# Scaling the handover blocks on DVE and ACT and turning them by transposes, in place of products with diag(factor)

## The chip, the cores and the metric

The kernel runs on one core of one Trainium2 chip. The metric is the device time of one execution in microseconds (us); several executions are taken and the median is given. Beside the timed runs there is one profiled execution, from which all rows of the profile come.

The engines by the names of the profile: PE is TensorE (matrix products), PEld its weight loads, DVE is VectorE, ACT is ScalarE, POOL is GpSimd, SP is SyncE, which here only issues DMAs. Each engine works through its own queue in order and waits on semaphores for the others.

## The reference

Two layers over 512 latent tokens and 256 context tokens of width 1024, all in float32. Layer 0 mixes tokens by retention, layer 1 by a gated linear recurrence (HGRN2); after each mixer comes a gated convolutional feed-forward. Around every one of these four sub-layers stands the same code, and the change lies only there:

```python
def rms_norm(x, g):
    xf = x.astype(jnp.float32)
    y = xf * lax.rsqrt(jnp.mean(xf * xf, -1, keepdims=True) + NORM_EPS)
    return (y * g.astype(jnp.float32)).astype(x.dtype)
...
        h_l = h_l + g1_l * rms_norm(y_l, norm_g[i, 1])
        u_l = rms_norm(h_l, norm_g[i, 2]) * (1.0 + sc2_l) + sh2_l
        h_l = h_l + g2_l * rms_norm(conv_ffn(u_l, ffn_w_up[i], ffn_conv_w[i], ffn_conv_b[i], ffn_w_down[i], True),
                                    norm_g[i, 3])
```

So the output y of a sub-layer is normalised, weighted and added to the stream h; then h is normalised again, scaled and shifted per channel, and is the input u of the next sub-layer.

## The kernel before

**Layout.** A sub-layer ends with tokens on the partitions: blocks of 128 tokens by 1024 channels. The next one needs its input u with channels on the partitions, as a sum of two float32r halves: hi (a rounded copy) and lo (the rest). Every large product is done three times (hi·hi, hi·lo, lo·hi).

**Handover.** The function `handover` is the bridge. It is used four times: after retention (called m0 in this document: 6 blocks, tiles named `trm`, `hxm`, `yr`, `um`), after the first feed-forward (e0: 6 blocks; `tre`, `hxe`, `yf`, `ue`), after the recurrence (m1: 4 blocks; again `trm`, `hxm`, and `yh`, `um`) and at the end (e1), which only writes the output and has no turn. In it `yb(b)` is the block of y in SBUF and `hb(b)` the block of the stream h.

For a block b, `norms` does, in this order: add the last partial product to y (DVE, L421), two sums of squares (ACT, L424), a reciprocal root r and one Newton step (ACT L428, DVE L142 to L144), y·r·gain (DVE, L448), h += y (DVE, L451) with a store of h to DRAM issued by POOL, the sum of squares of h (ACT, L452, which writes its squares over `yb`), the factor q by the same root and Newton step, and last the 128x128 matrix dg = diag(q) (DVE, L459).

For a pair of blocks, `turn` does four times (j = 0..3, two groups of 128 channels each): four float32 products of a 128x128 piece of `hb` with dg (PE, L475), which turn the piece and scale it by q at once, into one PSUM bank of 512 columns; two ACTs that apply the channel scale and shift out of PSUM (`mod`, L484) into a part of `yb`, whose content is no longer needed; hi (ACT, L491); lo (DVE, L492). The bank comes from a pool of two (`sml`), so group j waits until `mod` of group j-2 has read its bank.

**Order.** Around the handover, `tail` and `lead` put everything into one plan: the last products of the sub-layer that ends (PE, `tl`, L528), the norms and turns, the weight splits of the next sub-layer (ACT L585, DVE L589), and its first products (PE, `ld`, L121), which need all four lo of a pair. Each step carries an engine, an estimated cost, the steps that it needs, a rank and a slack. `Plan.run` plays this through once while the program is built: each engine takes, among the steps that its estimates call ready, the one of lowest rank. This fixes the order of instructions in the queues of PE, ACT and DVE; at run time they keep that order. A rank is a tuple: `(-1,)` goes ahead of all, `(-1, 9)` are the splits of the first weight half, then `(pr, stage)` of pair pr, `(1, 9)` the splits of the second half. On PE the turns have rank `(0,)`, the `tl` products rank 1, the `ld` products rank 2.

Of the kernel before, what the change touches and what calls it, by code (L numbers as in the profile page):

```python
# [9 lines left out]
F32 = mybir.dt.float32  # L10
F32R = mybir.dt.float32r
U8 = mybir.dt.uint8
AF = mybir.ActivationFunctionType
ALU = mybir.AluOpType

P = 128
# [22 lines left out]
class Plan:  # L39
# [5 lines left out]
    def add(self, eng, cost, deps, rank, emit, slack=0.0):  # L45
        self.steps.append(Step(eng, cost, list(deps), rank, emit, slack))
        return self.steps[-1]
# [22 lines left out]
class Net:  # L70
# [321 lines left out]
    def handover(self, nm, y, hsrc, gain, mods, u, hdst, nb, big, tmp):  # L392
        nc = self.nc
        per = y[0].shape[1]
        hx = [big([P, 3, D], F32, f"hx{nm}{j}") for j in range((nb + 2) // 3)]
        if nb % 3:
            g = hx[-1][:, 2:3]
        else:
            g = big([P, 3, D], F32, "gr" + nm)[:, 0:2]
        small = lambda n, w: self.cp.tile([P, w], F32, tag=f"sm{w}", name=f"{n}{nm}", bufs=12)  # L400
        rows = hsrc.rearrange("(b p) d -> p b d", p=P)
        for j, x in enumerate(hx):
            n = min(3, nb - 3 * j)
            nc.sync.dma_start(x[:, :n], rows[:, 3 * j : 3 * j + n])
        for v in range(g.shape[1]):
            nc.scalar.dma_start(g[:, v], self.gains[gain][v : v + 1].broadcast_to([P, D]))
        yb = lambda b: y[b // per][:, b % per]
        hb = lambda b: hx[b // 3][:, b % 3]
        if u is not None:
            A, B = mods()  # L410

        def norms(b, tails):
            ts, v, pr = slice(b * P, b * P + P), int(b >= 4), b // 2
            ss, r, q, dg = {}, {}, {}, {}
            add = self.plan.add
            half = lambda c: slice(c * 512, c * 512 + 512)

            def evac(c):
                if not c:
                    ss[0] = small(f"ss{b}", 4)  # L420
                nc.vector.tensor_tensor(yb(b)[:, half(c)], tails[c].ps, yb(b)[:, half(c)], ALU.add)  # L421

            def square(c):
                nc.scalar.activation(tmp(f"sq{nm}{b}{c}"), yb(b)[:, half(c)], AF.Square, accum_out=ss[0][:, c : c + 1])  # L424

            def start(d, x):
                d[0] = small(f"{'rq'[d is q]}{b}", 2)
                nc.scalar.activation(d[0][:, 0:1], x, AF.Abs_reciprocal_sqrt, bias=self.eps, scale=1.0 / D)  # L428

            sq = []  # L430
            for c in range(2):
                e = add("DVE", 0.67, [tails[c]], (pr, 0), lambda c=c: evac(c))
                tails[c].freed = e
                sq.append(add("ACT", 0.75, [e], (pr, 1), lambda c=c: square(c)))
            n = add("DVE", 0.16, sq, (-1,), lambda: nc.vector.tensor_tensor(ss[0][:, 2:3], ss[0][:, 0:1], ss[0][:, 1:2],
                                                                            ALU.add))
            n = add("ACT", 0.28, [n], (-1,), lambda: start(r, ss[0][:, 2:3]))
            n = add("DVE", 0.55, [n], (-1,), lambda: self.newton(r[0], ss[0][:, 2:3]))
            if u is None:
                for c in range(2):  # L440
                    cs = half(c)
                    n = add("DVE", 1.35, [n], (pr, 2), lambda cs=cs: (
                        nc.vector.scalar_tensor_tensor(yb(b)[:, cs], yb(b)[:, cs], r[0][:, 0:1], g[:, v, cs],  # L443
                                                       ALU.mult, ALU.mult),
                        nc.vector.tensor_tensor(hb(b)[:, cs], hb(b)[:, cs], yb(b)[:, cs], ALU.add),  # L445
                        (nc.sync, nc.scalar)[c].dma_start(hdst[ts, cs], hb(b)[:, cs])))
                return None
            n = add("DVE", 1.28, [n], (pr, 2), lambda: nc.vector.scalar_tensor_tensor(  # L448
                yb(b), yb(b), r[0][:, 0:1], g[:, v], ALU.mult, ALU.mult))
            n = add("DVE", 1.23, [n], (pr, 2), lambda: (  # L450
                nc.vector.tensor_tensor(hb(b), hb(b), yb(b), ALU.add), nc.gpsimd.dma_start(hdst[ts], hb(b))))  # L451
            n = add("ACT", 1.23, [n], (pr, 3), lambda: nc.scalar.activation(yb(b), hb(b), AF.Square,  # L452
                                                                           accum_out=ss[0][:, 3:4]))
            n = add("ACT", 0.28, [n], (-1,), lambda: start(q, ss[0][:, 3:4]))
            n = add("DVE", 0.55, [n], (-1,), lambda: self.newton(q[0], ss[0][:, 3:4]))

            def diag():
                dg[0] = self.cp.tile([P, P], F32, tag="diag", name=f"dg{nm}{b}", bufs=4)
                nc.vector.tensor_scalar(dg[0], self.ident, q[0][:, 0:1], None, ALU.mult)  # L459

            n = add("DVE", 0.25, [n], (-1,), diag)
            return n, dg

        def turn(pr, ready):
            add, v, cs = self.plan.add, int(pr == 2), slice(pr * W, pr * W + W)
            done = []
            for j in range(4):
                ps = {}

                def cross(j=j, ps=ps):  # L470
                    ps[0] = self.sml(f"tr{nm}{pr}{j}").rearrange("p (f t) -> p f t", f=2)
                    for f in range(2):
                        for z, (_, dg) in enumerate(ready):
                            k = 2 * j + f
                            nc.tensor.matmul(ps[0][:, f, z * P : z * P + P], hb(2 * pr + z)[:, k * P : k * P + P], dg[0],  # L475
                                             start=True, stop=True)

                x = yb(2 * pr + j // 2).rearrange("p (f t) -> p f t", f=4)[:, j % 2 * 2 : j % 2 * 2 + 2]
                hi, lo = (u[z + j // 2][:, j % 2 * 2 : j % 2 * 2 + 2, cs] for z in (0, 2))

                def mod(j=j, ps=ps, x=x):
                    for f in range(2):
                        k = 2 * j + f
                        nc.scalar.activation(x[:, f], ps[0][:, f], AF.Identity, scale=A[:, k, v : v + 1],  # L484
                                             bias=B[:, k, v : v + 1])

                prev = self.cross[-2:][:1] if len(self.cross) > 1 else []
                t = add("PE", 0.45, [n for n, _ in ready] + prev, (0,), cross, 1.0)
                m = add("ACT", 0.95, [t], (pr, 4), mod)
                self.cross.append(m)  # L490
                e = add("ACT", 0.62, [m], (pr, 5), lambda hi=hi, x=x: nc.scalar.activation(hi, x, AF.Copy))  # L491
                done.append(add("DVE", 0.67, [e], (pr, 6), lambda hi=hi, lo=lo, x=x: nc.vector.tensor_tensor(  # L492
                    lo, x, hi.bitcast(F32), ALU.subtract)))
            return done

        return norms, turn

    @staticmethod
# [939 lines left out]
```

## Time and profile before

| | us |
|---|---|
| timed runs | 2173.55, 2172.46, 2169.12 |
| median | 2172.46 |
| profiled execution | 2173.22 |
| its span in the profile | 2171.5 |
| busy: PE / DVE / ACT / POOL | 2113.8 / 1337.2 / 830.5 / 303.8 |

The span is the time from the first to the last recorded instruction; the execution's own time has 1.7 us more around it. The three handovers with a turn lie at about 676 to 747 us (m0), 1255 to 1326 us (e0) and 1755 to 1806 us (m1). In the profile one float32 product appears as two records on PE, so the 128 products of L475 are 256 records. "Idle before" in a row is the time in which the engine stood still just before those instructions, with the one that released it.

### The profile page before, as it was taken

The page shows a single profiled execution, that of the slowest core. Times are in us where ns is not written, and L with a number is a line of the kernel's source. Part 1 is how long each engine was busy: PE and PEld are TensorE (multiplying, and loading weights), DVE is VectorE, ACT ScalarE, POOL GpSimd, SP SyncE. Part 2 cuts the span into 40 slices and gives each one's busy share as a digit, 9 for nine tenths or more (in the row PEclk, how much of TensorE's full clock was granted, in tenths as well). Part 3 has the DMA queues.
Part 4 walks back from the last instruction along what each step waited for, and adds up shares of the span by engine and source line. Part 5 has one row for each costly group of instructions (what it writes and reads, how often), then busy time and mean ns, then how long its engine had stood idle before and what let it go on. Part 6 is the DMA issues. An engine that isn't in the chain of part 4 may idle for free. (4 is left out here: it accounts for less than half of the span.)

```text
span 2171.5 us, 31001 instructions
## 1 busy us (share of the span) xinstructions
PE 2113.8 (97%) x12416; PEld 1784.8 (82%) x12416; DVE 1337.2 (62%) x2536; ACT 830.5 (38%) x1615; POOL 303.8 (14%) x383
## 2 busy tenths in 40 slices
PE   6999999999999999999999999999999889999997
PEld 4888888888888988888888889888888668888886
DVE  6866565663613677467676576777777764334545
ACT  4542343423523723322132165434443454333323
POOL 4622040310100000000000003333333310000000
PEclk9999999999999999999999999999999999999999
DMA  9122314133123223333333532212121243223232
GB/s 297 40 78 98 108 40 145 59 112 132 64 93 125 99 98 108 126 116 124 112 110 125 175 112 73 59 40 59 40 59 40 78 168 122 92 97 97 92 114 95
DMA packets 186610, 218.25 MB, mean 101 GB/s; under 512 B 6113, under 2 KB 157665, under 8 KB 185697
## 3 DMA queue, kind: packets, MB, share of 16 engines
q1 hardware_dynamic: 179280, 196.80, 27.9%
q0 software_dynamic: 2736, 13.11, 1.6%
q10 hardware_dynamic: 4448, 6.35, 0.9%
q8 instruction: 98, 1.61, 0.3%
q14 instruction: 48, 0.39, 0.1%
HBM read 200.90 MB, written 15.34 MB: 100 GB/s over the span
## 5 line engine op out<-in xcount | busy, mean ns | idle before, releaser
L121 PE MATMUL f<-um,hua 128*128 128x512 f32 (+1 forms) x960 | 258.1, 356 | 0.0
L121 PE MATMUL f<-um,huv 128*128 128x512 f32 (+1 forms) x960 | 255.8, 354 | 0.0
L264 DVE SCALAR_TENSOR_TENSOR rows<-rada,sc,rows 128x256 f32<-128x256 f32 x504 | 231.7, 484 | 5.4
L1061 PE MATMUL f<-hd,gt 128*128 128x512 f32 x720 | 228.2, 396 | 0.0
L121 PEld LDWEIGHTS f<-um,hua 128*128 128x128 f32 x960 | 169.6, 189 | 29.3 <-issue 4.0
L121 PE MATMUL hp<-ue,hhw 128*128 128x512 f32 (+1 forms) x672 | 192.5, 373 | 0.0
L121 PEld LDWEIGHTS f<-um,huv 128*128 128x128 f32 x960 | 170.0, 189 | 25.2
L121 PE MATMUL f<-um,lua 128*128 128x512 f32 (+1 forms) x480 | 170.1, 354 | 0.0
L121 PE MATMUL f<-um,luv 128*128 128x512 f32 (+1 forms) x480 | 169.7, 354 | 0.0
L1061 PEld LDWEIGHTS f<-hd,gt 128*128 128x128 f32 x720 | 134.9, 187 | 33.6 <-issue 0.8
L1061 PE MATMUL f<-ld,gt 128*128 128x512 f32 x360 | 142.2, 395 | 0.0
L121 PEld LDWEIGHTS hp<-ue,hhw 128*128 128x128 f32 x672 | 112.2, 190 | 17.8 <-issue 1.4
L819 PE MATMUL v<-hv,ua 128*128 128x512 f32 x384 | 120.5, 390 | 0.0
L121 PE MATMUL hp<-ue,lhw 128*128 128x512 f32 (+1 forms) x336 | 120.1, 357 | 0.0
L121 PEld LDWEIGHTS f<-um,lua 128*128 128x128 f32 x480 | 90.7, 189 | 13.0
L121 PEld LDWEIGHTS f<-um,luv 128*128 128x128 f32 x480 | 90.7, 189 | 12.7
L1033 DVE TENSOR_TENSOR c<-f,c 128x512 f32<-128x512 f32 (+1 forms) x60 | 36.1, 601 | 100.4 <-PE f L121 100.4
L987 PE MATMUL wo<-hwo,ogr 128*128 128x512 f32 x288 | 89.3, 391 | 0.0
L1020 ACT ACTIVATE c<-f,c_conv_b,c_conv_w 128x512 f32<-128x512 f32 (+1 forms) x60 | 42.2, 703 | 118.6 <-PE f L121 118.6
L819 PEld LDWEIGHTS v<-hv,ua 128*128 128x128 f32 x384 | 72.1, 188 | 15.3 <-issue 0.6
L451 POOL DMA_DIRECT2D h_dram<-hxe x6 | 3.2, 531 | 576.2 <-DVE yf L421 542.5
L94 DVE TENSOR_TENSOR lua<-rua,hua 128x512 fp32r<-128x512 f32 x80 | 50.5, 685 | 53.6 <-ACT hua L93 53.4
(483 smaller groups left out, 4833.3 us busy)
## 6 DMA issues: line engine op xcount, KB each, us to landing
rada<-ada_w SPq DMA_DIRECT2D x48, 1024.0 KB
rua<-ffn_w_up SPq DMA_DIRECT2D x20, 1024.0 KB
ruv<-ffn_w_up SPq DMA_DIRECT2D x20, 1024.0 KB
rd<-ffn_w_down SPq DMA_DIRECT2D x24, 768.0 KB
rhw<-hg_w_in SPq DMA_DIRECT2D x28, 512.0 KB
rv<-ret_w_in SPq DMA_DIRECT2D x8, 1024.0 KB
rg<-ret_w_in SPq DMA_DIRECT2D x8, 1024.0 KB
rqk<-ret_w_in SPq DMA_DIRECT2D x6, 1024.0 KB
```

Source lines behind the costliest of these rows:

```text
L94: (eng or self.nc.vector).tensor_tensor(lo, raw, hi.bitcast(F32), ALU.subtract)
L121: nc.tensor.matmul(o, a, b[:, s], start=(i == 0), stop=(i == n - 1))
L264: nc.vector.scalar_tensor_tensor(rows[:, v], raw[:, k], a, rows[:, v], ALU.mult, ALU.add)
L451: nc.vector.tensor_tensor(hb(b), hb(b), yb(b), ALU.add), nc.gpsimd.dma_start(hdst[ts], hb(b))))
L819: nc.tensor.matmul(ps, a, b, start=(c == 0 and k == 0 and z == 0), stop=(c == 1 and k == 3 and z == 2))
L987: nc.tensor.matmul(ps, l, r[:, k], start=(h == 0 and k == 0 and z == 0), stop=(h == 2 and k == 3 and z == 2))
L1020: nc.scalar.activation(c[:, s], ps, AF.Identity, bias=cb[:, i, mt : mt + 1], scale=w(1))
L1033: nc.vector.tensor_tensor(c[:, s], ps, c[:, s], ALU.mult)
L1061: nc.tensor.matmul(ps, l, r[:, k], start=(k1 + k == 0 and z == 0), stop=(k1 + k == nt - 1 and z == 2))
```

## The change

The factor q is no longer put into a diagonal matrix. Each block of h is multiplied by its q into `yb` (the squares there are not needed): columns 0 to 511 by DVE, columns 512 to 1023 by ACT. PE then turns the scaled pieces by transposes against the constant identity. Groups j = 0, 1 read the half of DVE, j = 2, 3 that of ACT. `mod` now writes its result into `hb`. The new steps have rank `(pr, 3)`, where the diagonal had `(-1,)`; the turn's estimated cost goes from 0.45 to 0.35 and its slack from 1.0 to 0.7.

```diff
@@ def norms(b, tails)
-            ss, r, q, dg = {}, {}, {}, {}
+            ss, r, q = {}, {}, {}
...
             n = add("DVE", 0.55, [n], (-1,), lambda: self.newton(q[0], ss[0][:, 3:4]))
 
-            def diag():
-                dg[0] = self.cp.tile([P, P], F32, tag="diag", name=f"dg{nm}{b}", bufs=4)
-                nc.vector.tensor_scalar(dg[0], self.ident, q[0][:, 0:1], None, ALU.mult)
-
-            n = add("DVE", 0.25, [n], (-1,), diag)
-            return n, dg
+            return [add("DVE", 0.65, [n], (pr, 3), lambda: nc.vector.tensor_scalar(
+                        yb(b)[:, half(0)], hb(b)[:, half(0)], q[0][:, 0:1], None, ALU.mult)),
+                    add("ACT", 0.65, [n], (pr, 3), lambda: nc.scalar.activation(
+                        yb(b)[:, half(1)], hb(b)[:, half(1)], AF.Copy, scale=q[0][:, 0:1]))]
@@ def turn(pr, ready)
                     for f in range(2):
-                        for z, (_, dg) in enumerate(ready):
+                        for z in range(2):
                             k = 2 * j + f
-                            nc.tensor.matmul(ps[0][:, f, z * P : z * P + P], hb(2 * pr + z)[:, k * P : k * P + P], dg[0],
-                                             start=True, stop=True)
+                            nc.tensor.transpose(ps[0][:, f, z * P : z * P + P], yb(2 * pr + z)[:, k * P : k * P + P],
+                                                self.ident)
 
-                x = yb(2 * pr + j // 2).rearrange("p (f t) -> p f t", f=4)[:, j % 2 * 2 : j % 2 * 2 + 2]
+                x = hb(2 * pr + j // 2).rearrange("p (f t) -> p f t", f=4)[:, j % 2 * 2 : j % 2 * 2 + 2]
...
-                t = add("PE", 0.45, [n for n, _ in ready] + prev, (0,), cross, 1.0)
+                t = add("PE", 0.35, [n[j // 2] for n in ready] + prev, (0,), cross, 0.7)
```

## The prediction

> **What bounds the kernel now.** I read the page first, then the busy time by stage over the three handovers, then the chain of work that ended last, then the timeline around the turns.
>
> ```profile
> span 2171.5 us, 31001 instructions
> PE 2113.8 (97%) x12416; PEld 1784.8 (82%) x12416; DVE 1337.2 (62%) x2536; ACT 830.5 (38%) x1615; POOL 303.8 (14%) x383
> ...
> core 0: us, PE busy (x) PEld busy (x) DVE busy (x) ACT busy (x) POOL busy (x), PEclk, DMA share, GB/s
> 676.00:747.00 71.00, 71.00 (x459) 64.75 (x459) 43.96 (x96) 43.51 (x99) 3.25 (x6) 1.00 0.36 127
> 1255.00:1326.00 71.00, 71.00 (x463) 64.25 (x462) 45.91 (x101) 44.11 (x100) 3.19 (x6) 1.00 0.31 101
> 1755.00:1806.00 51.00, 45.68 (x281) 39.91 (x280) 33.28 (x70) 28.98 (x67) 3.48 (x6) 0.97 0.49 175
> ```
>
> PE is the bound. In m0 and e0 it never stops (71.00 of 71.00 us) while DVE and ACT are busy for some 44 to 46 us: what leaves PE there shortens the kernel. m1 is different: PE lacks 5.3 us. Its waits, and the records of the turns:
>
> ```profile
> L475 PE MATMUL trm<-dgm,hxm 128*128 128x128 f32 x64 | 9.5, 313 | 3.8 <-DVE dgm L459 3.8
> L121 PE MATMUL ld<-um,hfl 128*128 128x256 f32 x128 | 24.0, 287 | 1.5 <-DVE um L492 1.0 <-ACT um L491 0.6
> ...
> L475 PE MATMUL trm<-dgm,hxm x160: 270/275/439, 703.7 to 1802.2; 128*128 128x128 f32 x160
> L475 PE MATMUL tre<-dge,hxe x96: 270/275/275, 1282.9 to 1322.0; 128*128 128x128 f32 x96
> ...
> 1782.76 3.00 PE trm L475 x14
> 1796.04 1.78 PE trm L475 x16
> ```
>
> The waits are all in m1's first pair, where PE runs out of `tl` products before q of block 1 exists. Everywhere else PE pays for every record of a turn.
>
> **The change part by part.** *The products become transposes.* 256 records stand for 128 products, two each; 16 records in a row cost 1.78 us of PE, 0.111 each (the 275 ns of one record overlap with the next). A float32 transpose of the same form, at the same clock, stands elsewhere in this trace:
>
> ```profile
> L1234 PE MATMUL ht<-c_ident,AK x80: 272/273/330, 1372.6 to 1743.6; 128*128 128x128 f32 x80
> 1740.82 0.44 PE ht L1234 x4
> ```
>
> The recurrence makes 8 heads x 10 = 80 such transposes in 80 records, so one record each; four take 0.44 us, 0.110 each. A turned piece thus goes from 0.222 to 0.110. A group of four saves 0.45, a pair of blocks (16 pieces) 1.78 us. m0 and e0 have three pairs each: 3 x 1.78 = **5.3 us each**. m1's second pair saves **1.8**. m1's first pair saves nothing directly, since PE waits on both sides of it.
>
> The Trainium skill ("TensorE: Matmul & The Clock Gate", Terms) calls transpose mode four times faster for FP32. By that a piece would cost 0.055 us, and the seven pairs would save 7 x 16 x 0.167 = 18.7 us. The row of 0.110 decides against it.
>
> *The scalings replace the diagonals.* No row shows a one-input DVE scaling of 128x512, so I bound it:
>
> ```profile
> L459 DVE TENSOR_SCALAR dgm<-c_ident,q1m x2: 276/282/288, 701.8 to 1782.4; 128x128 f32<-128x128 f32 x2
> L262 DVE TENSOR_SCALAR rows<-rada,sc x72: 339/349/532, 94.8 to 1234.8; 128x256 f32<-128x256 f32 x72
> L589 DVE TENSOR_TENSOR lfl<-rfl,hfl 128x512 fp32r<-128x512 f32 x8 | 5.2, 685 | 0.0
> L585 ACT ACTIVATE hfl<-rfl x16: 612/617/632, 708.7 to 1783.8; 128x512 fp32r<-128x512 f32 x16
> ```
>
> Below: 0.35, the 256-column row; above: 0.69, the 512 columns with two inputs. The step from 128 to 256 columns, 0.07, continued twice more gives 0.49; I take 0.5. Against the diagonal's 0.28 that is +0.22 a block (+0.07 to +0.41), 3.5 us over 16 blocks. ACT gets a copy of 128x512, 0.62, 16 times: 9.9 us. In m0 and e0 both lie in the 25 to 28 us that these engines have free in each stage. The question is whether a turn comes late:
>
> ```profile
> 701.81 0.28 DVE L459 TENSOR_SCALAR dgm<-c_ident,q1m 128x128 f32<-128x128 f32 x1
> 717.60 0.28 DVE L459 TENSOR_SCALAR dgm<-c_ident,q3m 128x128 f32<-128x128 f32 x1
> 733.36 0.28 DVE L459 TENSOR_SCALAR dgm<-c_ident,q5m 128x128 f32<-128x128 f32 x1
> 703.72 1.95 PE L475 MATMUL trm<-dgm,hxm 128*128 128x128 f32 x16
> 721.23 1.95 PE L475 MATMUL trm<-dgm,hxm 128*128 128x128 f32 x16
> 736.31 1.95 PE L475 MATMUL trm<-dgm,hxm 128*128 128x128 f32 x16
> ```
>
> In m0 the three diagonals are ready 1.6, 3.3 and 2.7 us before PE comes to the turn. A scaling that ends 0.22 later (DVE) or 0.34 later (ACT, and only needed for j = 2, 3) stays inside; so does the 1.78 by which each earlier pair brings PE forward, as the norms hang on `tl` products that come forward too. If that cover went, PE would stand still by the difference: below 1 us a turn. The planned cost and slack sum to the same as before (0.65 + 0.7 against 0.25 + 1.0), up to 0.1.
>
> *m1's first pair* is a chain, not a queue. q of block 1, scaling, turn, `mod`, hi, lo, then `ld`:
>
> ```profile
> 1783.82 0.61 ACT L585 ACTIVATE hfl<-rfl 128x512 fp32r<-128x512 f32 x1
> 1784.34 1.00 ACT L484 ACTIVATE yh<-trm,mod,mv1A 128x256 f32<-128x256 f32 x2
> 1785.78 1.02 ACT L484 ACTIVATE yh<-trm,mod,mv1A 128x256 f32<-128x256 f32 x2 [0.44 <-PE trm L475]
> 1787.73 1.93 ACT L484 ACTIVATE yh<-trm,mod,mv1A 128x256 f32<-128x256 f32 x4
> 1791.57 0.39 PE L121 MATMUL ld<-um,hfl 128*128 128x256 f32 x1 [0.95 <-DVE um L492]
> ```
>
> ACT works through it almost without a gap. It gains the 0.44 for which it waited on the slow products (1785.78) and pays 0.62 for the scaling of block 1: **+0.2**, between -0.9 (the copy falls in another gap) and +0.9 (both additions count in full).
>
> *`mod` writes into `hb`* and so waits for the store of that block of h, which POOL issued. Behind it on ACT are hi and the next splits, and PE's `ld` waits for those.
>
> ```profile
> 1790.08 0.53 POOL L451 DMA_DIRECT2D h_dram<-hxm  x1 [10.63 <-DVE hxm L451]
> 1796.96 1.93 ACT L484 ACTIVATE yh<-trm,mod,mv1A 128x256 f32<-128x256 f32 x4 [3.83 <-PE trm L475]
> DMA to landing us min/median/max: 2.9/2.9/5.6
> ```
>
> The shortest distance from a store to the `mod` that will write its block is this one, 6.9 us. A store lands in 2.9 us, at most 5.6. Cost nothing; without that cover, what is missing of the landing. No DMA is moved. The tile of h is now held until the last lo, that of y only until the last transpose; the next stage's first loads follow the last lo either way.
>
> *The sum*, against the profiled execution (2173.2 us, its span 2171.5 plus 1.7, 0.8 above the median 2172.46): -5.3 - 5.3 - 1.8 + 0.2 = -12.2. **2161.0 us**, 0.56% less. About 0.2%, 4.3 us, can be told from no change.
>
> **The rivals.** *B, the clock stays low in m1.* After the wait of 3.8 us the granted clock fell, and came back while the products ran:
>
> ```profile
> 1783.00:1784.00 1.00, 1.00 (x7) 1.00 (x7) 0.93 (x6) 1.00 (x5) 0.00 (x0) 0.60 0.38 156
> 1784.00:1785.00 1.00, 1.00 (x7) 1.00 (x6) 0.93 (x5) 1.00 (x3) 0.00 (x0) 0.50 0.02 8
> 1786.00:1787.00 1.00, 1.00 (x8) 1.00 (x8) 1.00 (x2) 1.00 (x3) 0.00 (x0) 0.70 0.00 0
> ```
>
> With half the records, that stretch loads PE less. If the clock then stays at half through the `ld` products from 1791.57 on for as long as it did before (about 3.5 us), half of that is lost: 1.7, and up to 2.5 with the start of `ld`. 2163.0. For it: the fall is in the rows. Against: the `ld` products between also work. The Trainium skill ("TensorE: Matmul & The Clock Gate", Part 4) says that transposes do not count as busy for the clock gate. By that rule this case comes for certain; no row here shows transposes alone for long enough.
>
> *C, a turn slips one slot.* The scaling has rank (pr, 3) where the diagonal went ahead of all, so the plan may put a turn behind one more `ld` product. In the last pair of m0 or e0 there is then one product (24 records at 0.12, 2.9 us) less between the turn and the `ld` that needs its lo: 2.9 us of waiting each, both 5.8: 2167. A third in m1 puts it near 2170.
>
> *D, slower: ACT stands before a step that isn't ready.* The order is fixed; already one split blocks ACT in m1 for 2.45 us, with the squares of block 1 behind it:
>
> ```profile
> 1776.36 2.45 issue
> 1778.81 1.15 ACT hfl L585 x2
> ```
>
> A rank of (pr, 3) behind the splits' (-1, 9) can produce this at other turns. At all eight it would cost 8 x 2.45 = 19.6, less 12.4 saved: +7, 2180. It decides from 12.4 / 8 = 1.55 us a turn. Against: in m0 and e0 PE has 1.6 us and more in hand.
>
> *E, better order.* The same reshuffle could free block 1's squares in m1 from that split: up to 2.45 and the clock's fall with it. 2157.5.
>
> *F, nothing won.* If these transposes also took two records, PE would gain nothing: 2173.4. The 80 records speak against it.
>
> **How the numbers follow.** A 0.48, B 0.13, C 0.17 (half of it within 0.2%), D 0.08, E 0.10, F 0.04. Faster by over 0.2%: 0.48 + 0.13 + 0.10 + 0.09 = 0.80; within: 0.08 + 0.04 = 0.12; slower: 0.08. The range runs from 2156.0 (E with the low end of the scalings) to 2168.5, which leaves out D, F and half of C, 0.20.
>
> **What would show it.** L475 with 128 records, 16-record runs of 1.78 replaced by 8-record runs of 0.89; m0 and e0 with PE still busy throughout and some 5.3 us shorter; in m1 PE's wait before the turn unchanged to half a microsecond, `ld` after the first pair at its old distance. DVE scaling near 0.5, ACT's near 0.62. Wrong if PE shows waits in m0 or e0, if the transposes run in two records, if `mod` waits on a DMA, or if the granted clock stays at 0.5 past the first `ld` products of m1.

## The result

The changed kernel takes 2159.38 us (median of 6 runs, 2157.03 to 2160.22) against 2173.01 (6 runs, 2169.12 to 2175.94). The ratio is 0.9938, with a 95% interval of 0.9927 to 0.9948: 13.6 us less where 12.2 were forecast, and inside the forecast range. Run again beside the last experiments it took 2159.34 us, ratio 0.9939 (0.9927 to 0.9952).

The page of the changed kernel, its span and busy times:

```profile
span 2155.3 us, 30784 instructions
PE 2096.5 (97%) x12288; PEld 1767.7 (82%) x12288; DVE 1340.6 (62%) x2536; ACT 840.0 (39%) x1631; POOL 304.5 (14%) x383
```

PE has 128 records and 17.3 us of busy time less, ACT 9.5 us more, DVE 3.4 more. That is the trade that the forecast counted: in m0 and e0 only PE had no room.

To see where the time went, cut each trace at the first `tl` product of a handover and at the first product of the next stage behind the `ld` products (tile `f` after m0 and m1, `hv` after e0). Both are start times in the rows of a tile; for m0 before and after (start of the first and of the last record stand behind the durations):

```profile
L528 PE MATMUL tl<-hwot,og x96: 389/389/476, 679.2 to 715.3; 128*128 128x512 f32 x96
L121 PE MATMUL f<-um,hua x96: 277/335/496, 757.2 to 799.2; 128*128 128x512 f32 x48, 128*128 128x256 f32 x48
```
```profile
L526 PE MATMUL tl<-hwot,og x96: 388/389/476, 677.5 to 711.7; 128*128 128x512 f32 x96
L121 PE MATMUL f<-um,hua x96: 278/336/497, 750.0 to 792.0; 128*128 128x512 f32 x48, 128*128 128x256 f32 x48
```

| length in us | m0 | e0 | m1 | recurrence between e0 and m1 |
|---|---|---|---|---|
| before | 78.0 | 73.2 | 61.6 | 424.3 |
| changed | 72.5 | 67.7 | 59.7 | 422.6 |
| changed, run again | 72.5 | 67.7 | 61.2 | 422.0 |

m0 and e0 are 5.5 us shorter each (forecast 5.3), m1 1.9 or 0.4 (forecast 1.6). These sum to 12.9 or 11.4. The spans of the profiled executions differ by more, by 16.2 and 14.3 us, and the medians by 13.6. The rest lies where the change touches nothing: m0 began anywhere from 677.3 to 679.2, and the recurrence took 421.6 to 426.0 us over all kernels of this study. In the recurrence the length goes with the clock that TensorE was granted: 421.6 and 422.0 us in the two executions in which it stayed at 1.00, 422.6 to 423.6 in the four with 3.4 us at half, 424.0 to 424.4 in the six with 6.8, and 426.0 in the one with 10.2. So 0.7 to 2.2 of the 13.6 us can't be put down to the change, and that the total came this near to the forecast is partly luck.

The turns of the changed kernel, and the chain of work that ended last:

```profile
L473 PE MATMUL trm<-c_ident,yr x48: 270/272/273, 702.0 to 735.5; 128*128 128x128 f32 x48
L473 PE MATMUL trm<-c_ident,yh x32: 270/286/475, 1764.7 to 1786.0; 128*128 128x128 f32 x32
L473 PE MATMUL tre<-c_ident,yf x48: 270/273/273, 1275.8 to 1309.5; 128*128 128x128 f32 x48
1781.64 0.87 PE trm L473 x8
```

One record a piece, eight in 0.87 us, where sixteen took 1.78: half a pair saves 0.91, and six halves 5.5 us. The durations in the rows (272 against 275 ns) hardly changed; they overlap, and only the distance of the starts is paid.

The changed kernel's m0, e0 and m1 by engine, up to the landmarks of the table; the first two rows begin some 3 us ahead of the handover (columns as in the prediction):

```profile
674.30:750.00 75.70, 75.70 (x495) 69.36 (x495) 51.03 (x106) 52.81 (x114) 3.25 (x6) 1.00 0.34 123
1247.90:1318.20 70.30, 70.30 (x455) 63.49 (x454) 49.84 (x105) 52.40 (x114) 3.22 (x7) 1.00 0.35 114
1740.80:1800.50 59.70, 53.54 (x339) 46.84 (x338) 38.45 (x77) 37.33 (x80) 2.97 (x5) 0.94 0.43 151
```

In m0 and e0 PE is still busy to the last hundredth, though ACT and DVE do more. m1 keeps its waits: 6.2 us without PE, where 5.3 were before.

### The profile page after: what moved, and what is told of

Read it like the earlier page. It is cut to its first block, busy times and chain, and to the rows that moved or that the text cites. A ratio compares the mean times of both kernels' runs of the same rounds, so it can differ in the third digit from the quotient of the medians.

```text
span 2155.3 us, 30784 instructions
## 1 busy us (share of the span) xinstructions
PE 2096.5 (97%) x12288; PEld 1767.7 (82%) x12288; DVE 1340.6 (62%) x2536; ACT 840.0 (39%) x1631; POOL 304.5 (14%) x383
## 5 line engine op out<-in xcount | busy, mean ns | idle before, releaser
L121 PEld LDWEIGHTS f<-um,huv 128*128 128x128 f32 x960 | 170.1, 189 | 25.1
L93 ACT ACTIVATE hua<-rua 128x512 fp32r<-128x512 f32 x80 | 44.2, 621 | 102.2 <-DMA rua<-ffn_w_up 53.2
```

The lines of the kernel that those rows point to most:

```text
L93: self.nc.scalar.activation(hi, raw, AF.Copy)
L121: nc.tensor.matmul(o, a, b[:, s], start=(i == 0), stop=(i == n - 1))
```

## The experiments

All times are medians; each kernel has its ratio to the kernel before on the same chip in the same session. Runs that the text comes back to are called e2, e3, e5, e8 and e9; e0 and e1 remain the handovers.

### Turning by products again

The scalings stay, the transposes become float32 products with the identity.

```diff
-                            nc.tensor.transpose(ps[0][:, f, z * P : z * P + P], yb(2 * pr + z)[:, k * P : k * P + P],
-                                                self.ident)
+                            nc.tensor.matmul(ps[0][:, f, z * P : z * P + P], yb(2 * pr + z)[:, k * P : k * P + P],
+                                             self.ident, start=True, stop=True)
```

> Blocks scaled as in the change, but turned by float32 products with the identity, two records a piece. Theory A (PE pays for every record of a turn, seven of eight pairs lie on its path): L475's 256 records are back, 112 pieces x 0.111 = 12.4 us more than the changed kernel, 2171.8 us. Rival (the gain came from the new order of the plan, or from the missing diagonals): 2159 to 2161 us.

2172.26 us, ratio 1.0002 (0.9993 to 1.0011): the whole gain is gone. m0 takes 77.9 and e0 73.1 us, the lengths of before. With everything else of the change in place, the 128 extra records are the difference.

### Every transpose twice

```diff
-                        for z in range(2):
+                        for z in (0, 1, 0, 1):
```

> Each transpose is issued twice, the second over the first. Theory A: 128 more records of 0.110 us, of which the 16 of m1's first pair may hide in its waits: 12.3 to 14.1 us over the changed kernel, 2171.7 to 2173.5 us. Rival (PE has room at the turns): 2159 to 2165 us.

This kernel, e3, took 2172.62 us, ratio 1.0001 (0.9992 to 1.0009), 13.2 over the changed kernel: 128 records, 0.10 us each. m0 took 77.7 us and e0 72.9, 5.2 more each. What a record less saved, a record more costs again, so PE has no slack at the turns of m0 and e0.

### Only the plan's numbers

```diff
-            n = add("DVE", 0.25, [n], (-1,), diag)
+            n = add("DVE", 0.65, [n], (pr, 3), diag)
...
-                t = add("PE", 0.45, [n for n, _ in ready] + prev, (0,), cross, 1.0)
+                t = add("PE", 0.35, [n for n, _ in ready] + prev, (0,), cross, 0.7)
```

> The kernel before with only the plan's numbers of the change: the diagonal at rank (pr, 3) and 0.65, the turn at 0.35 with slack 0.7. Theory A: PE's work is the same, 2172 to 2174 us. Rival (the new order brings the gain): down towards 2160 us.

2173.15 us, ratio 1.0004 (0.9995 to 1.0013). The new costs and ranks bring nothing by themselves.

### No scaling at all, twice

To price the scalings they were left out: the transposes read h itself, q is missing from the result, and `mod` writes to y as before.

```diff
-            return [add("DVE", 0.65, [n], (pr, 3), lambda: nc.vector.tensor_scalar(
...
+            return [n, n]
```

> Transposes straight from h, the factor q is left out and no scaling is done. Theory A: the scalings lie beside PE's work in m0 and e0 and cost a few tenths in m1, so 2158 to 2159.5 us. Rival (the scalings are on the path of every turn, 0.2 to 0.6 us each): 2154 to 2157 us.

This kernel, e2, took 2170.95 us, ratio 0.9991 (0.9982 to 1.0): less work, and 11.6 us *slower* than the changed kernel. Both theories missed. The timeline of PE in the last pair of its handover e0 shows why:

```profile
1314.16 1.03 PE L470 MATMUL tre<-c_ident,hxe 128*128 128x128 f32 x8
1317.39 0.66 PE L470 MATMUL tre<-c_ident,hxe 128*128 128x128 f32 x4 [2.19 <-ACT yf L479]
1318.30 0.66 PE L470 MATMUL tre<-c_ident,hxe 128*128 128x128 f32 x4 [0.25 <-ACT yf L479]
1319.55 0.39 PE L121 MATMUL ld<-ue,hhl 128*128 128x256 f32 x1 [0.34 <-DVE ue L487]
1321.15 0.38 PE L121 MATMUL ld<-ue,hhl 128*128 128x256 f32 x1 [0.75 <-ACT ue L486]
1321.88 0.39 PE L121 MATMUL ld<-ue,hhl 128*128 128x256 f32 x1 [0.34 <-DVE ue L487]
```

Between the two halves of this turn stands no `ld` product any more. With two steps less the plan came to another order, in which all the `ld` products of the first two pairs go ahead of the last turn, and PE has nothing with which to cover `mod`, hi and lo: 3.9 us of waits. In the changed kernel the two halves start at 1304.94 and 1308.69, with one `ld` product (2.9 us) between them. m0 shows the same with 2.4 us of waits; it took 76.2 us and e0 72.9, against 72.5 and 67.7. This execution, 2166.24 us, was the fastest of the eleven. What the others took beyond it stands in no trace; their mean granted clock was 0.987 to 0.993 against 0.995. e2 thus removed two things at once. The clean form (e5) keeps the two steps in the plan, with cost and rank, and lets them issue nothing:

```diff
+            return [add("DVE", 0.65, [n], (pr, 3), lambda: None),
+                    add("ACT", 0.65, [n], (pr, 3), lambda: None)]
```

> As e2 (transposes straight from h, q left out), but the plan keeps the two scaling steps with their costs and ranks; they only issue nothing. Theory A (e2 lost its time to the other order of the plan, the scalings themselves lie beside PE's work): like the changed kernel, 2157.5 to 2159.5 us, with PE free of waits in m0 and e0. Rival (turns without the scaling are slower for another reason, such as the results going to y instead of h): 2166 to 2171 us as e2.

2160.69 us, ratio 0.9943 (0.9931 to 0.9956), 1.2 over the expected range. m0 takes 72.4 and e0 67.7 us, as with the scalings. Its profiled execution, 2159.0 us, lies 2.0 above that of the changed kernel, and m1 has it: 61.9 us, with the clock at half for 13.7. So the twelve scalings of m0 and e0 on each engine, 5.8 us of DVE (12 x 0.48) and some 8.5 of ACT (12 x 0.71), cost nothing measurable, and `mod` writing to y instead of h makes no difference there.

### All of it on DVE

DVE scales the whole block, ACT's step issues nothing.

```diff
-                        yb(b)[:, half(0)], hb(b)[:, half(0)], q[0][:, 0:1], None, ALU.mult)),
-                    add("ACT", 0.65, [n], (pr, 3), lambda: nc.scalar.activation(
-                        yb(b)[:, half(1)], hb(b)[:, half(1)], AF.Copy, scale=q[0][:, 0:1]))]
+                        yb(b), hb(b), q[0][:, 0:1], None, ALU.mult)),
+                    add("ACT", 0.65, [n], (pr, 3), lambda: None)]
```

> The whole block is scaled by DVE (about 0.9 us instead of 0.48), ACT scales nothing; the plan's numbers stay. Theory A (both engines have room): within 1.5 us of the changed kernel, 2158 to 2161 us. Rival (the split in halves is what keeps the turns in time): 16 x 0.4 us on the path, 2164 to 2166 us.

2161.3 us, 0.3 over the expected range, ratio 0.9947 (0.9934 to 0.9959); the interval overlaps that of the changed kernel (0.9927 to 0.9948). DVE's scaling of 128x1024 took 0.75 us. m0 takes 72.8, e0 67.8, m1 60.0 us. The division in halves is at most worth a microsecond or two, and not shown to be worth anything.

### m1: the wait and the clock

In m1's first pair PE waits for block 1. The timeline of PE there in the changed kernel, and the granted clock (PEclk, the third number from the end):

```profile
1764.65 0.30 PE L473 MATMUL trm<-c_ident,yh 128*128 128x128 f32 x1 [0.25 <-DVE yh L457]
1769.56 1.73 PE L473 MATMUL trm<-c_ident,yh 128*128 128x128 f32 x7 [4.60 <-DVE ss3m L435]
1771.69 2.02 PE L473 MATMUL trm<-c_ident,yh 128*128 128x128 f32 x8 [0.40 <-ACT hxm L482]
1776.46 0.39 PE L121 MATMUL ld<-um,hfl 128*128 128x256 f32 x1 [0.64 <-DVE um L490]
```
```profile
1768.00:1769.00 1.00, 0.00 (x0) 0.00 (x0) 0.86 (x8) 1.00 (x5) 0.00 (x0) 0.60 0.75 303
1774.00:1775.00 1.00, 0.88 (x4) 0.88 (x5) 1.00 (x2) 1.00 (x3) 0.00 (x0) 0.50 0.91 373
1775.00:1776.00 1.00, 0.75 (x4) 0.35 (x3) 1.00 (x3) 1.00 (x3) 0.50 (x1) 0.99 0.00 0
```

The row names ss3m, the instruction behind DVE's scaling of block 1 (1768.93 to 1769.41); the scaling is what the turn needs. The clock was at half from about 1768.2 to 1775.0, nearly 7 us, twice as long as before, but it was back before PE's last wait (until 1776.46) was over. It cost little: with products in the gap, below, the clock never fell in m1, and m1 took the same 59.7 us. In the second profiled execution of the same kernel it came back later:

```profile
1776.00:1778.00 2.00, 1.57 (x6) 1.27 (x7) 2.00 (x5) 2.00 (x5) 0.38 (x1) 0.50 0.55 225
1778.00:1780.00 2.00, 2.00 (x12) 2.00 (x11) 1.86 (x8) 1.58 (x5) 0.00 (x0) 0.50 0.13 45
1780.00:1782.00 2.00, 2.00 (x17) 2.00 (x17) 0.88 (x3) 1.00 (x2) 0.00 (x0) 0.89 0.80 215
```

There the clock was at half from 1770.2 to 1780.4, the `ld` products ran at half until then, and m1 took 61.2 instead of 59.7 us. This is what rival B describes, in one of two executions. Do transposes keep the clock up? PE's gap was filled once with forty repeats of a transpose, once with twenty float32 products (40 records):

```diff
+                    for _ in range(40 if (nm, pr, j) == ("m1", 0, 0) else 0):
+                        nc.tensor.transpose(ps[0][:, 0, 0:P], yb(0)[:, 0:P], self.ident)
```

> In m1's first pair PE repeats one transpose of block 0 forty times (4.4 us) while it waits for block 1. If transposes count as work for the clock: the granted clock stays near 1.0 through the turns and the first lead products, and the time is the same or up to 1 us lower, 2158 to 2160 us. If they don't: the clock falls to 0.5 as without them.

> The same gap filled with twenty float32 products (40 records, 4.4 us). Products kept the clock up elsewhere, so the granted clock should stay near 1.0 through the gap whichever way the transposes come out; 2158 to 2160 us. If the clock falls here too, the gap is cold for another reason.

The gap filled with transposes (PE's timeline, then the clock), and last the clock with products in the gap:

```profile
1767.24 4.56 PE L471 MATMUL trm<-c_ident,yh 128*128 128x128 f32 x40 [0.24 <-DVE yh L457]
1772.15 0.96 PE L475 MATMUL trm<-c_ident,yh 128*128 128x128 f32 x7 [0.25 <-DVE ss3m L435]
1774.29 0.66 PE L475 MATMUL trm<-c_ident,yh 128*128 128x128 f32 x4 [1.18 <-ACT hxm L484]
```
```profile
1770.00:1772.00 2.00, 1.91 (x18) 1.67 (x16) 1.86 (x11) 2.00 (x7) 0.00 (x0) 1.00 0.63 252
1774.00:1776.00 2.00, 1.46 (x9) 1.02 (x9) 2.00 (x3) 2.00 (x5) 0.53 (x1) 1.00 0.04 8
1778.00:1780.00 2.00, 1.33 (x6) 1.13 (x7) 2.00 (x4) 2.00 (x5) 0.53 (x1) 0.82 0.45 184
```
```profile
1768.00:1770.00 2.00, 2.00 (x20) 2.00 (x19) 1.71 (x9) 2.00 (x9) 0.00 (x0) 1.00 0.82 323
1776.00:1778.00 2.00, 1.10 (x7) 0.91 (x8) 2.00 (x5) 2.00 (x4) 0.53 (x1) 1.00 0.32 133
```

From 1767.2 to 1773.1 PE ran transposes alone, and the clock stayed at 1.00, also afterwards until 1779.3. With PE idle there, it had fallen 3.3 us after the end of the last record (1764.95 to 1768.2), and 4.9 us after it in the second execution (1765.3 to 1770.2). So transposes do keep the clock up here, in one profiled execution; products did the same (1.00 throughout m1). The Trainium skill ("TensorE: Matmul & The Clock Gate", Part 4) says that transposes don't count as busy for the clock; this run says otherwise, and it decides. The times, 2160.66 us (0.9943, 0.9931 to 0.9956; 0.7 over the expected range) and 2159.84 (0.9941, 0.9928 to 0.9955), show no gain: PE then waited 1.18 us for the bank and further on for lo, and in the kernel with the transposes the clock fell after those waits, at 1779.3, for 3.4 us.

### Another order for m1

PE's wait of 4.6 us hangs on ACT, which stands before a split that can't run until the last `tl` product has read its weights, with the squares of block 1 behind it. Two kernels change the plan only; the second also takes away the lead that the first half's splits have over the norms of the first pair.

```diff
-            e = add("ACT", 0.6, [freed[z], got], (-1 if z == 0 else 1, 9), hi)
+            e = add("ACT", 0.6, [freed[z], got], (-1 if z == 0 else 1, 9), hi, 2.0 * z)
```
```diff
-            (-1 if z == 0 else 1, 9)
+            (z, 9)
```

> The changed kernel itself, once more, as the measure for the two orders beside it: 2158.5 to 2160.5 us.

> The changed kernel, with 2 us of slack in the plan for the splits of the second weight half, so that in m1 the squares of block 1 come before them on ACT. Theory A (ACT stands before a split that waits for the last tl product, and PE's wait in m1 hangs on that): PE's wait before the first turn of m1 falls from 4.6 to some 2.5 us, 1.5 to 2.5 us less in all, 2157 to 2158 us. Rival (the chain through ACT takes as long anyway): no difference to the changed kernel.

> As e8, and the splits of the first weight half no longer go ahead of the first pair's norms. Theory A: block 1's h comes another 1 to 2 us sooner in m1; 2155.5 to 2158 us, if m0 and e0 keep PE free of waits. Rival (the splits come late for the first lead products): PE waits in m0 and e0, 2160 us and more.

e8, the first: 2158.6 us (0.9934, 0.9922 to 0.9947). PE's wait before block 1 is down from 4.6 to 2.5 us as expected, but the time is not down by the 1.5 to 2.5 us: beside the changed kernel's 2159.34 it can't be told apart. The next waits had grown, from 0.40 to 1.21 us for `mod` and from 0.64 to 0.98 for lo, and the clock was at half for 10.2 us; m1 took 60.0. e9, the second: 2157.12 us (2155.91 to 2157.32), ratio 0.9927 (0.9914 to 0.9941), inside the expected range; its five runs all lie below the five of the changed kernel beside it (2158.91 to 2160.17), by 2.2 us at the median, though the intervals of the ratios overlap. In the traces m1 is 59.2 us against 59.7 and 61.2. m0 and e0 take 72.5 and 67.7 us without a wait of PE. In m1 PE's wait for block 1 is 1.5 us:

```profile
1766.74 0.95 PE L473 MATMUL trm<-c_ident,yh 128*128 128x128 f32 x7 [1.53 <-DVE yh L457]
1768.52 0.66 PE L473 MATMUL trm<-c_ident,yh 128*128 128x128 f32 x4 [0.82 <-ACT hxm L482]
1771.50 0.58 PE L121 MATMUL ld<-um,hfl 128*128 128x256 f32 x1 [0.98 <-DVE um L490]
```
```profile
1774.00:1777.00 3.00, 3.00 (x16) 3.00 (x15) 1.47 (x9) 3.00 (x9) 0.00 (x0) 0.50 0.43 173
```

But the clock falls here too, from 1770.7 to 1777.6, and the `ld` products run at half for some 6 us. What an order without that fall would take was not tried.

## Why the prediction was right

**The products.** The forecast rested on one comparison, 16 records in 1.78 us against four transposes in 0.44. Measured: 5.5 us each for m0 and e0 against 5.3. That it is the records, and not the order or the diagonals, is shown from three sides: products back (12.9 us back), transposes doubled (13.2 us), plan alone (nothing). This step carried 10.6 of the forecast 12.2 us, and it is right in its mechanism and in its size.

**The scalings.** DVE's took 0.48 us (0.5 taken), ACT's more than its row:

```profile
L457 DVE TENSOR_SCALAR yr<-hxm,q1m x1: 479/479/479, 700.1 to 700.1; 128x512 f32<-128x512 f32 x1
L459 ACT ACTIVATE yr<-hxm,q1m x1: 724/724/724, 699.1 to 699.1; 128x512 f32<-128x512 f32 x1
```

0.71 to 0.73 where 0.62 was taken from a copy without a scale per partition. It changed nothing in m0 and e0, as both lie beside PE's work; with the same plan and no scaling the time did not fall. In m0 the first scaled pair was ready at 700.6 and PE came to it at 702.0, with 1.4 us in hand where the diagonal had 1.6.

**m1's first pair** was forecast at +0.2 and came to about -0.1 in one execution and +1.4 in the other (m1's -1.9 and -0.4, with the 1.8 forecast for the second pair taken out). That the forecast lies between them is partly luck, for the parts are not those of the forecast. Cut m1 where PE ends its wait for block 1, and again where it ends its last wait for a lo of the first pair:

| us | to the turn | to the last lo | to the end of m1 |
|---|---|---|---|
| before | 27.7 | 8.8 | 25.1 |
| changed | 28.8 | 6.9 | 24.0 |
| changed, run again | 28.7 | 6.9 | 25.6 |

The first part grew, mainly because PE's wait before the turn went from 3.8 to 4.6 us: DVE's scaling, now at rank (pr, 3), stands behind a Newton step of block 2 (three instructions, 0.5 us) and is 0.2 longer than the diagonal. The plan's numbers alone already give 4.4, so most of it is the plan's order. The second part fell by 1.9 where the forecast had +0.2. ACT no longer waited 0.44 for products. With products still in place this part takes 7.6 us with the plan's numbers alone and 7.8 in the kernel that turns by products again, so about half of the 1.9 came with the new order. The third part has the saving of the second pair, and here the clock decides: the two executions of one program differ by 1.6 us, with the clock at half until 1775.0 in one and until 1780.4 in the other. The forecast named this as rival B, at 1.7 to 2.5 us, because half the records load PE less. The traces bear that out as far as they go: where the first pair's turn has 32 records (before, plan alone, products again, every transpose twice), the clock was back 3.7 to 3.9 us after PE came out of its wait; with 16 (the two executions of the changed kernel, e2, e5, all on DVE, e8) it took 5.5 to 11.4 us. No run changes this alone. Transposes as such are not the reason: issued twice they brought the clock back as early as products did, and in the filled gap they kept it up.

**The signs.** Most of what the prediction said would show it came out: 128 records, PE without a wait in m0 and e0, runs of eight in 0.87 us, DVE near 0.5. Four signs did not, of which three lie in m1: PE's wait before the turn moved by 0.8 us and not within half a microsecond, the way from the turn to the last lo was 1.9 us shorter, the clock was still at half for the first `ld` products, for 1.6 us in one execution and over 6 in the other, and ACT's scaling took 0.71 and not 0.62. In its numbers two things do not follow from what stands beside them: no row gives the -0.9 for the first pair, and the low end of the range, taken as E with that bound, is 2156.4 and not 2156.0.

**The store.** `mod` writes into h and might have waited for the store of h. The waits of ACT in m1, by what ended them (total, times, longest):

```profile
ACT hxm L482 <- PE trm L473: 2.2, 2, 1.5
ACT hfl L583 <- issue: 1.8, 1, 1.8
```

`mod` (L482) waits for PE alone; no DMA ends a wait of it there, nor in m0 or e0. A store landed in at most 5.7 us.

**The rivals.** C, one `ld` product less behind a turn, did not come with the change; in e2 no such product was left, at 3.9 us in e0 where 2.9 was the price of one. D's stall of ACT stayed the one that there was (1.8 us against 2.45). E, a better order, was not what the change brought; e9 had to be made for it, and gave 2.2 of the 3.5 us that E counted on.

## What to carry to other kernels

Where one engine is busy without a gap through a stage, count its records and price each by the distance of starts in a run of them. Work moved to engines with room in that stage can then be free, as it was in m0 and e0 here; both can be tested by doubling one and dropping the other. A stage where that engine waits, as m1, has to be priced as a chain of its own. When an order is planned from estimated costs, an experiment that drops an instruction must keep its step in the plan, or it measures another order: e2 lost 11.6 us with less work, and e5, with the step kept, gained them back but for a microsecond. A float32 product with a diagonal that only scales and turns costs two records here, a transpose one.

## What the runs showed of the hardware

A copy on ACT with a scale per partition took 0.71 to 0.73 us for 128x512, without one 0.62. DVE's product with a factor per partition took 0.28 us for 128 columns (the diagonal), 0.48 for 512 and 0.75 for 1024. A float32 product of 128x128 by 128x128 showed as two records on PE, a transpose as one, each 0.11 us from start to start.

The granted clock fell to half not only in PE's wait of 4.6 us (3.3 us after its last record in one execution, 4.9 in the other, when PE had just begun again). In the kernel with doubled transposes it fell 1.5 us after the last record, and in e9 after waits of 1.5, 0.8 and 0.4 us within 5.5 us, with PE busy for about half of that time. In m1 it then stayed at half for 3.4 us before the change, 6.8 and 10.2 in two executions of the changed kernel, and 13.7 in e5; with twice the records in the turn it was back sooner, 3.7 to 3.9 us after PE resumed against 5.5 to 11.4. The recurrence, which the change does not touch, was 422 us long without such a fall and up to 426 with 10.2 us of it: a difference of 2 us between two kernels can be this alone, and the row of the clock for the untouched stages shows it.
